# A planner's table of engine costs re-fitted: TensorE's rate, fixed parts, GpSimd's rate and an idle clock

## The chip, the core and the metric

The kernel runs on one core of a Trainium2 chip as one program. The metric is the device time of one execution in microseconds, as the median of a few runs. A core has five instruction queues: TensorE (PE in the profile, with its weight loads as PEld), VectorE (DVE), ScalarE (ACT), GpSimd (POOL) and SyncE (SP, here for DMAs alone). Each queue is worked off in the order in which the program holds it.

## The reference, cut to what matters

A two-layer diffusion backbone in float32, with 512 latent tokens (`x`) and 256 context tokens (`ctx`), 1024 wide, FFN width 2816. Each layer is a half-step SwiGLU FFN, a mixer, and a second half-step FFN, each behind a modulated RMSNorm:

```python
mod_l = (silu(c) @ w_mod[i] + b_mod[i])          # 9 x 1024, the same for ctx with c_ctx
x = x + 0.5 * mod[2] * swiglu(modulate(rmsnorm(x), mod[0], mod[1]), w13, w2)
x = x + mod[5] * mixer(modulate(rmsnorm(x), mod[3], mod[4]))
x = x + 0.5 * mod[8] * swiglu(modulate(rmsnorm(x), mod[6], mod[7]), w13, w2)
```

The mixer of layer 0 is a bidirectional S5 state-space scan beside a multi-scale pooling of windows; that of layer 1 is a bidirectional gated DeltaNet of 8 heads in chunks, with a triangular solve for each chunk. At the end stands a final RMSNorm of `x`.

## The kernel before

The work is one long stream of weight slabs (128 x 1024), in the order of the layers. SP loads a slab, ACT rounds it to the matmul's format (`whi`), DVE or POOL forms what the rounding left (`wlo`), and PE multiplies it in three passes (`whi` by `hhi`, `whi` by `hlo`, `wlo` by `hhi`) with tokens as columns. Stages in order of the span: first FFN (to about 640 us), S5 and pooling mixer (to about 960), second FFN of layer 0 and first of layer 1 (to about 2000), DeltaNet mixer (to about 2660), last FFN. The FFNs after the first use seven products in place of eight, with extra sums on DVE.

Beside the main stream run side threads. In the first FFN one makes the modulation rows (`mods`, L535: a row of 1024 products with a sum, tile `mscr` on DVE, started at least `MP` = 5000 ns apart, L69, L584 and L2608; 56 rows for two streams), and one builds the S5 tables (`tables`, L1307: tiles `z` and `s5u` on DVE and POOL, then transposes of `z` and products on PE). In the DeltaNet mixer (`mixer1`, L1906) the main thread projects 24 tiles, then 8 more, while threads work on each head: `conv` (L2049, DVE; tiles `kT`, `qT`, `sqsum`), `norms` (L2075; `kn` scaled on POOL), `pre` (L2125; loads `E`, masks it on POOL, makes the matrices `NT` and `aq`), `subst` and `loop` (L2209 and L2241; a triangular substitution of 31 steps with two POOL instructions each, `s5l` and `xm`), `levels` (L2288; tiles `fX`, `fP`, `fQ` on 32 or 64 partitions) and four `scan` threads (L2363; tiles `u`, `O`, in a chain of PE, DVE and ACT).

No order is written out by hand. Class `Flow` (L78) is a list planner that runs while the program is built. Each stage is a Python generator. `run` (L237) always goes on with the thread that can start first, by the planner's own clock; what that thread issues is appended to the engines' queues, so the order of these calls is the program order of every queue. Each issued instruction passes through `engine` (L197, the call at L206, which is why every instruction of the profile has this line) to `account` (L130). There the instruction starts when its engine is free and its operands are ready (`ready`, L121: the end of the write plus a hop from `HOP`, L87: 197 ns after PE, 142 after ACT, 127 after DVE, 105 after POOL), and takes `c` ns from a table by engine, operation, size and type. `account` sees all of PE, ACT, DVE, POOL and DMAs; the result changes no instruction, only what is called next. `flag` (L460) lets a thread go on only when what it needs is done by the planner's PE time, and the free PSUM bank is chosen by planned use (L297). Some waits are numbers in planner time: the pace of the modulation rows above, `MPS` = 9000 for those of layer 1.

The two lines of the table that price PE and POOL are these:

```python
c = max(n / 2.4 * (1 if ins[-1].dtype == F32R else 2 if op == "transpose" else 4), 27.0)
c = n * 0.83 + 140.0 if op == "affine_select" else n / 1.2 + 60.0 if op == "memset" else n * 2.05 + 145.0
```

Here `n` is the number of elements in a partition of the output. The functions that the diff touches follow.

Of the kernel before, what the change touches and what calls it, by code (L numbers as in the profile page):

```python
# [11 lines left out]
F32R = mybir.dt.float32r  # L12
# [6 lines left out]
P = 128  # L19
# [58 lines left out]
class Flow:  # L78
# [11 lines left out]
    def __init__(self):  # L90
        self.free = dict.fromkeys(("tensor", "scalar", "vector", "gpsimd", "sync"), 0.0)
        self.dma = self.sent = 0.0
        self.writes = {}
        self.bank_of = {}
        self.bank_used = [0.0] * 8
        self.held = [False] * 8
        self.chunk_banks = []
        self.flags = {}
        self.threads = []
        self.now = self.end = 0.0  # L100
        self.table = 0
        self.first = {}
        self.cost = {}
        self.used = self.last = self.uset = None
        self.tabs = {}
# [24 lines left out]
    def account(self, eng, op, a, k):  # L130
        self.used = self.used or eng
        aps = [v for v in (*a, *k.values()) if isinstance(v, bass.AP)]
        outs = [aps[0]] + ([k["accum_out"]] if k.get("accum_out") is not None else [])
        ins = [v for v in aps[1:] if v is not k.get("accum_out")]
        t = max(self.free[eng], *(self.ready(v, eng) for v in aps))
        n = 1
        for s in aps[0].shape[1:]:
            n *= s
        if op == "dma_start":
            b = 4.0  # L140
            for s in aps[0].shape:
                b *= s
            if eng == "gpsimd":
                self.free[eng] = t + 1040.0
                t += 1040.0
            else:
                self.free[eng] = t + 60.0
                t += 1100.0
            self.dma = max(self.dma, t) + b / 360.0
            self.sent = self.dma + 900.0  # L150
            self.note(aps[0], self.sent, "dma")
            return
        banks = [self.bank_of[v.tensor.name] for v in aps if v.tensor.name in self.bank_of]
        if eng == "tensor":
            c = max(n / 2.4 * (1 if ins[-1].dtype == F32R else 2 if op == "transpose" else 4), 27.0)
        elif eng == "scalar":
            c = n / 1.2 + (51.0 if ins[0].tensor.name in self.bank_of else 93.0)
            c += 93.0 * (len(outs) > 1 or isinstance(k.get("scale"), bass.AP) or isinstance(k.get("bias"), bass.AP))
            s = self.TABLE.get(k.get("func", a[2] if len(a) > 2 else None))
            self.uset = self.uset or s  # L160
            if s and s != self.table:
                self.table = s
                c += 1283.0
        elif eng == "vector":
            m = 1
            for s in ins[0].shape[1:] if ins else ():
                m *= s
            two = op in ("tensor_tensor", "tensor_add", "tensor_sub", "tensor_mul", "tensor_max")
            c = max(n, m) / 0.96 + (69.0 if two or len(ins) < 2 else 130.0)
            if op == "scalar_tensor_tensor" and not isinstance(a[2] if len(a) > 2 else k.get("scalar"), bass.AP):  # L170
                c -= 61.0
            if op in ("tensor_scalar", "tensor_copy") and not banks:
                c -= n / 1.92
        else:
            c = n * 0.83 + 140.0 if op == "affine_select" else n / 1.2 + 60.0 if op == "memset" else n * 2.05 + 145.0
        t += c
        self.free[eng] = t
        for v in outs:
            self.note(v, t, eng)
        for b in banks:  # L180
            self.bank_used[b] = max(self.bank_used[b], t)
        if t > self.end:
            self.end, self.last = t, eng
# [2620 lines left out]
```

## Time and profile before

| what | value |
|---|---|
| runs, us | 3003.7, 2997.89, 3007.39 (median 3003.7) |
| profiled execution, us | 2999.02 |
| its span, us | 2997.2 |
| mean granted TensorE clock | 0.968 |
| PE / DVE / ACT / POOL busy, share of span | 93% / 69% / 41% / 24% |
| HBM read, written | 308.10 MB, 45.25 MB |

The profile shows one execution. A line of it names engine, operation, output tile, input tiles, how often, busy time and mean time of one, then the idle time of the engine before these instructions and who ended it. "PE ps <- POOL kn" among the waits means that PE stood idle, with a matmul that writes a PSUM tile next in its queue, until POOL had written `kn`. The granted clock is a share of full speed.

### The profile page before, as it was taken

The numbers are of one execution on the slowest core, as the hardware profiler recorded it, in microseconds if no ns is written. First come the engines' busy times: TensorE is split into PE (matmuls) and PEld (weight loads), VectorE is DVE, ScalarE is ACT, GpSimd is POOL, SyncE is SP. The second block draws the span as 40 slices with busy tenths as digits, with TensorE's granted clock in tenths as the row PEclk, the third lists the DMA queues.
The fourth block names the chain that finished last, engine by engine and source line by source line (L and its number), as shares of the span: only waits on it lengthen the run. The fifth ranks groups of instructions, "written<-read, shape, count | busy, mean of one in ns | idle before, by whom it ended". The sixth has DMA issues, their size and how long they took to land.

```text
span 2997.2 us, 47031 instructions
## 1 busy us (share of the span) xinstructions
PE 2774.2 (93%) x18380; PEld 2520.0 (84%) x18380; DVE 2060.3 (69%) x3941; ACT 1242.2 (41%) x2464; POOL 708.5 (24%) x1210
## 2 busy tenths in 40 slices
PE   7999989999999999999999999998778888889998
PEld 3787778888888999988999998897667777789977
DVE  6878763256837788753779895367667776678845
ACT  3221212224336444422544443236665766455532
POOL 1244521031212000010201111022764474100011
PEclk9999999999999999999999999999889999899999
DMA  6544442222421544442155665222111133224441
GB/s 233 164 158 163 154 143 70 65 68 82 120 55 41 197 157 146 164 152 79 43 185 168 211 231 202 80 81 88 47 43 49 34 103 114 102 75 134 139 160 57
DMA packets 99247, 356.41 MB, mean 119 GB/s; under 512 B 12448, under 2 KB 16192, under 8 KB 97360
## 3 DMA queue, kind: packets, MB, share of 16 engines
q1 hardware_dynamic: 57552, 192.12, 19.5%
q0 software_dynamic: 38144, 157.09, 15.8%
q10 hardware_dynamic: 3328, 4.20, 0.4%
q8 instruction: 144, 2.36, 0.3%
q14 instruction: 79, 0.65, 0.1%
HBM read 308.10 MB, written 45.25 MB: 118 GB/s over the span
## 4 chain that ended last, share of the span: by engine, by line
PE 66%; DVE 10%; POOL 9%; issue 6%; DMA 6%; ACT 3%; POOLq 0%; DVEq 0%; SPq 0%; ACTq 0%
PE ps L206 66%; POOL xm L206 2%; POOL s5l L206 2%; POOL z L206 2%; DMA E<-gd 2%; DVE wlo L206 1%; POOL s5u L206 1%; DVE mscr L206 1%; DMA wf<-in_wmodf_dram 1%; DVE xT L206 1%; DMA grffn<-gdffn 1%; DVE rsq_a L206 1%; DVE nt L206 1%; DMA z<-in_s5c_dram 1%; DVE h7l L206 1%
## 5 line engine op out<-in xcount | busy, mean ns | idle before, releaser
L206 DVE TENSOR_TENSOR wlo<-raw,whi 128x1024 fp32r<-128x1024 f32 (+1 forms) x310 | 352.3, 1138 | 352.6 <-ACT whi L206 351.9
L206 ACT ACTIVATE whi<-raw 128x1024 fp32r<-128x1024 f32 (+1 forms) x324 | 316.0, 978 | 652.3 <-PE ps L206 641.9
L206 PE MATMUL ps<-hhi,whi 128*128 128x256 f32 (+1 forms) x1304 | 457.3, 351 | 0.5 <-ACT gg L206 0.5
L206 PE MATMUL ps<-hlo,whi 128*128 128x256 f32 (+1 forms) x1304 | 441.0, 338 | 1.4 <-DVE hlo L206 1.4
L206 PE MATMUL ps<-hhi,wlo 128*128 128x256 f32 (+1 forms) x1304 | 440.1, 337 | 2.0 <-DVE wlo L206 1.4
L206 PE MATMUL ps<-h7h,whi 128*128 128x256 f32 (+1 forms) x976 | 298.6, 314 | 4.6 <-ACT whi L206 4.0
L206 PE MATMUL ps<-h7h,wlo 128*128 128x256 f32 (+1 forms) x976 | 297.4, 313 | 4.9 <-DVE wlo L206 4.8
L206 PE MATMUL ps<-ghffn,wlo 128*128 128x256 f32 (+1 forms) x896 | 296.3, 331 | 5.5 <-DVE wlo L206 5.5
L206 PE MATMUL ps<-h7h,sh 128*128 128x384 f32 (+1 forms) x960 | 293.3, 318 | 6.9 <-ACT cffn L206 6.8
L206 PE MATMUL ps<-ghffn,whi 128*128 128x256 f32 (+1 forms) x896 | 297.5, 332 | 0.4 <-ACT ghffn L206 0.4
L206 PE MATMUL ps<-glffn,whi 128*128 128x256 f32 (+1 forms) x896 | 297.2, 332 | 0.6 <-DVE glffn L206 0.6
L206 PE MATMUL ps<-h7h,sl 128*128 128x384 f32 (+1 forms) x960 | 293.1, 317 | 3.4 <-DVE sl L206 3.4
L206 DVE SCALAR_TENSOR_TENSOR xT<-ps,gate,xT 128x256 f32<-128x256 f32 (+1 forms) x352 | 195.1, 578 | 128.3 <-PE ps L206 124.0
L206 PEld LDWEIGHTS ps<-hhi,wlo 128*128 128x128 f32 x1304 | 251.2, 193 | 31.3 <-DVE wlo L206 1.8
L206 PEld LDWEIGHTS ps<-hhi,whi 128*128 128x128 f32 x1304 | 252.2, 193 | 27.0 <-issue 1.2
L206 PEld LDWEIGHTS ps<-hlo,whi 128*128 128x128 f32 x1304 | 252.5, 194 | 25.0 <-DVE hlo L206 2.0
L206 PE MATMUL ps<-h7l,whi 128*128 128x256 f32 (+1 forms) x976 | 217.9, 313 | 2.1 <-DVE h7l L206 2.1
L206 ACT ACTIVATE cffn<-ps 128x384 f32<-128x384 f32 (+1 forms) x300 | 131.7, 451 | 197.6 <-PE ps L206 196.4
L206 POOL TENSOR_TENSOR sqsum<-sqsum,sq 128x256 f32<-128x256 f32 x96 | 78.2, 815 | 557.8 <-ACT sq L206 476.4
L206 PEld LDWEIGHTS ps<-h7h,wlo 128*128 128x128 f32 x976 | 188.2, 193 | 6.0 <-DVE wlo L206 5.7
L206 PEld LDWEIGHTS ps<-h7h,whi 128*128 128x128 f32 x976 | 188.2, 193 | 5.5 <-ACT whi L206 4.4
L206 PEld LDWEIGHTS ps<-ghffn,wlo 128*128 128x128 f32 x896 | 169.2, 189 | 23.7 <-DVE wlo L206 6.7
(350 smaller groups left out, 6396.3 us busy)
## 6 DMA issues: line engine op xcount, KB each, us to landing
raw<-in_ffn_dram SPq DMA_DIRECT2D x264, 512.0 KB
xT<-in_wmod_dram POOLq DMA_DIRECT2D x72, 512.0 KB, 4.6
wm<-in_wmod_dram POOLq DMA_DIRECT2D x56, 512.0 KB, 4.2
raw<-in_gin_dram SPq DMA_DIRECT2D x33, 512.0 KB
grffn<-gdffn POOLq DMA_DIRECT2D x40, 384.0 KB, 4.2
gdffn<-cffn POOLq DMA_DIRECT2D x36, 384.0 KB, 2.6
wf<-in_wmodf_dram POOLq DMA_DIRECT2D x16, 512.0 KB, 7.9
xd<-xT POOLq DMA_DIRECT2D x2, 3072.0 KB, 11.1
```

The costliest lines, as they stand in the source:

```text
L206: r = f(*a, **k)
```

## The change

Only the planner's table is changed, and one field is added. No instruction, tile, wait or DMA is added or taken out; what can change is the order of the instructions in each queue, and the times in planner time at which paced steps come up.

- PE: products in the rounded format go from N/2.4 to N/2.2 ns, doubled below 256 columns; float32 products get 10 ns more and a floor of 54 in place of 27; transposes go from N/1.2 with that floor to N/1.2 + 3 with a floor of 30.
- PE when idle: after more than 3400 ns without an instruction, everything that starts in the 4500 ns that follow is priced twice.
- ACT: the fixed part goes from 51 to 78 ns with a PSUM source, from 93 to 113 otherwise; 110 more on fewer than 128 partitions.
- DVE: 18 ns more for each instruction, 90 more on fewer than 128 partitions, 350 more for a transpose of 512.
- POOL: two-operand instructions go from 2.05 N + 145 to 2.5 N + 200, selects from 0.83 N + 140 to N + 168, memsets from N/1.2 + 60 to N + 72.

Hops, DMA prices and paces stay as they are.

```diff
--- before.py
+++ after.py
@@ -97,7 +97,7 @@
         self.chunk_banks = []
         self.flags = {}
         self.threads = []
-        self.now = self.end = 0.0
+        self.now = self.end = self.cold = 0.0
         self.table = 0
         self.first = {}
         self.cost = {}
@@ -152,9 +152,18 @@
             return
         banks = [self.bank_of[v.tensor.name] for v in aps if v.tensor.name in self.bank_of]
         if eng == "tensor":
-            c = max(n / 2.4 * (1 if ins[-1].dtype == F32R else 2 if op == "transpose" else 4), 27.0)
+            if op == "transpose":
+                c = max(n / 1.2 + 3.0, 30.0)
+            elif ins[-1].dtype == F32R:
+                c = n / 2.2 * (2 if n < 256 else 1)
+            else:
+                c = max(n / 0.6 + 10.0, 54.0)
+            if t - self.free[eng] > 3400.0:
+                self.cold = t + 4500.0
+            if t < self.cold:
+                c *= 2
         elif eng == "scalar":
-            c = n / 1.2 + (51.0 if ins[0].tensor.name in self.bank_of else 93.0)
+            c = n / 1.2 + (78.0 if ins[0].tensor.name in self.bank_of else 113.0) + (110.0 if aps[0].shape[0] < P else 0.0)
             c += 93.0 * (len(outs) > 1 or isinstance(k.get("scale"), bass.AP) or isinstance(k.get("bias"), bass.AP))
             s = self.TABLE.get(k.get("func", a[2] if len(a) > 2 else None))
             self.uset = self.uset or s
@@ -171,8 +180,9 @@
                 c -= 61.0
             if op in ("tensor_scalar", "tensor_copy") and not banks:
                 c -= n / 1.92
+            c += 18.0 + (90.0 if aps[0].shape[0] < P else 0.0) + (350.0 if op == "transpose" and n == 512 else 0.0)
         else:
-            c = n * 0.83 + 140.0 if op == "affine_select" else n / 1.2 + 60.0 if op == "memset" else n * 2.05 + 145.0
+            c = n + 168.0 if op == "affine_select" else n + 72.0 if op == "memset" else n * 2.5 + 200.0
         t += c
         self.free[eng] = t
         for v in outs:
```

## Rows read from the trace of the kernel before

**Rows 1.** The page, part 1: busy us (share of span) and instructions of each engine.
```profile
PE 2774.2 (93%) x18380; PEld 2520.0 (84%) x18380; DVE 2060.3 (69%) x3941; ACT 1242.2 (41%) x2464; POOL 708.5 (24%) x1210
```

**Rows 2.** Stretches: from:to, length, busy us (instructions), granted clock, DMA share, GB/s.
```profile
60.00:440.00 380.00, 350.51 (x2114) 303.27 (x2113) 311.51 (x555) 87.71 (x138) 146.68 (x177) 0.97 0.48 155
440.00:640.00 200.00, 200.00 (x1210) 175.51 (x1209) 69.09 (x98) 43.67 (x64) 14.80 (x20) 1.00 0.22 70
1050.00:1250.00 200.00, 200.00 (x1152) 200.00 (x1151) 174.47 (x266) 89.01 (x139) 16.65 (x31) 1.00 0.44 147
2000.00:2680.00 680.00, 559.61 (x4459) 495.26 (x4458) 482.90 (x1042) 412.39 (x1091) 303.68 (x642) 0.92 0.22 74
2100.00:2250.00 150.00, 116.81 (x1032) 102.34 (x1033) 99.23 (x207) 97.33 (x268) 102.26 (x221) 0.85 0.13 44
2700.00:2840.00 140.00, 140.00 (x1213) 140.00 (x1213) 123.09 (x188) 82.62 (x145) 7.02 (x13) 1.00 0.41 132
```

**Rows 3.** Waits of PE in 60:440: us in total, times, longest us.
```profile
PE ps L206 <- DVE z L206: 17.9, 6, 6.3
PE ps L206 <- POOL z L206: 9.5, 5, 2.5
```

**Rows 4.** Waits of PE in 2000:2680, columns as before.
```profile
PE ps L206 <- POOL kn L206: 20.0, 5, 7.7
PE ps L206 <- DVE u L206: 17.9, 6, 8.4
PE ps L206 <- ACT qT L206: 16.0, 1, 16.0
PE ps L206 <- DVE O L206: 8.3, 5, 4.4
PE ps L206 <- ACT u L206: 7.3, 5, 2.9
PE ps L206 <- DVE NT L206: 6.9, 2, 4.5
PE ps L206 <- ACT O L206: 5.8, 7, 1.6
PE ps L206 <- ACT fQ L206: 2.6, 1, 2.6
PE ps L206 <- DVE fP L206: 1.9, 3, 0.7
```

**Rows 5.** POOL by shape, 2050:2550: count, busy us, mean ns, idle before it.
```profile
L206 POOL TENSOR_SCALAR_AFFINE_SELECT E<-E 128x768 f32<-128x768 f32 x16 | 16.2, 1014 | 66.5 <-DMA E<-gd 66.5
L206 POOL TENSOR_TENSOR s5l<-lm,xm 128x126 f32<-128x126 f32 x24 | 14.0, 583 | 1.7
L206 POOL TENSOR_TENSOR s5l<-lm,xm 128x120 f32<-128x120 f32 x16 | 11.8, 740 | 1.0
L206 POOL TENSOR_TENSOR s5l<-lm,xm 128x110 f32<-128x110 f32 x16 | 8.9, 558 | 1.0
L206 POOL TENSOR_TENSOR kn<-kn,rsq_r 128x768 f32<-128x768 f32 x8 | 12.6, 1580 | 21.5 <-DVE rsq_r L206 21.5
```

**Rows 6.** POOL by shape, 60:440, columns as in rows 5.
```profile
L206 POOL TENSOR_TENSOR z<-z,s5u 128x128 f32<-128x128 f32 x14 | 13.7, 980 | 1.0
```

**Rows 7.** DVE and ACT by shape, 2000:2680, columns as in rows 5.
```profile
L206 DVE SCALAR_TENSOR_TENSOR u<-ps,neG,nv 128x128 f32<-128x128 f32 x80 | 26.7, 345 | 19.6 <-PE ps L206 18.7
...
L206 ACT ACTIVATE u<-ps 128x128 f32<-128x128 f32 x112 | 28.6, 273 | 37.4 <-PE ps L206 37.0
L206 ACT ACTIVATE fX<-lm 32x192 f32<-32x192 f32 x48 | 17.3, 360 | 9.4 <-DVE lm L206 8.6
```

**Rows 8.** DVE by shape, 60:440, columns as in rows 5.
```profile
L206 DVE SCALAR_TENSOR_TENSOR mscr<-wm,cbc 128x1024 bf16<-128x1024 f32 x112 | 147.7, 1319 | 16.1 <-DMA wm<-in_wmod_dram 14.4 <-DVE gg L206 0.4 <-ACT cbc L206 0.2
L206 DVE DVE_READ_ACCUMULATOR mscr<-wm,cbc 128x1 f32 x112 | 9.2, 82 | 0.0
```

**Rows 9.** The chain that ended last, 2060:2240: shares of the stretch by line.
```profile
by line: PE ps L206 25.5%; issue 15.3%; POOL xm L206 15.3%; POOL s5l L206 15.0%; DMA E<-gd 13.4%; DVE wlo L206 2.9%; POOL E L206 2.9%; POOL kn L206 2.4%; DVE NT L206 2.3%; DVE sqsum L206 1.8%; DVE lm L206 1.6%; DVE qT L206 1.1%; DVE aq L206
```

## The prediction

> **What bounds the kernel now.** I read the page's busy line first, then the stretches by stage, then what TensorE (PE) waits for in the stages where it stands idle, then the durations of the instructions behind those waits. The busy line shows PE at 93% of 2997.2 us [rows 1], so 223 us of the span have no matmul in flight, and only this part can move: the diff changes no instruction, only the order in which each engine's queue holds them. The stretches show where the idle time is [rows 2]. In 440-640, 1050-1250 and 2700-2840 PE is busy for the whole stretch at a granted clock of 1.00: no other order can help there. In the first FFN (60-440) PE is busy 350.5 of 380 us, so 29.5 us are idle. In the DeltaNet mixer (2000-2680) it is busy 559.6 of 680 us, so 120 us are idle, and the granted clock is 0.92 there, 0.85 in 2100-2250. What is left, about 73 us, lies in the first 60 us, in the norms between stages and at the end, where a chain has nothing beside it.
>
> What PE waits for in these two stretches is not the stream of weights but side work that stands in its queue ahead of ready matmuls. In the first FFN it is the S5 tables: 17.9 us for z from VectorE (DVE) and 9.5 us for z from GpSimd (POOL) [rows 3], almost all of the 29.5. In the mixer it is the heads' chains: kn from POOL 20.0, u 17.9, qT 16.0, O 8.3 and so on, 86.7 us in the nine rows that stand here [rows 4]. PE takes its queue in order, so each is a place where the planner thought that the side chain would be done by the time PE got there. That is what the table of costs decides.
>
> **The change part by part.**
>
> *PE's rate* (N/2.4 to N/2.2 columns per ns). In 1050-1250 the matmuls have 384 columns: 1152 in 200 us, 173.6 ns each, 2.21 columns per ns; in 2700-2840 they have 256: 1213 in 140 us, 115.4 ns each [rows 2]. The old table says 160 and 106.7, the new one 174.5 and 116.4. The new one is right within 1%, the old one 8% short. In saturated stretches this changes nothing in time (cost 0; what hides it is that PE never waits there, and without that cover a slab split laid later would show as a wait of PE on wlo, of which these stretches have none; I keep 0). Elsewhere it means that the planner counts 9% fewer main matmuls passing during a side chain of given length, so a side chain's own PE steps move forward in PE's queue unless the chain's prices rise as much.
> The Trainium skill's page "TensorE: Matmul & The Clock Gate", section "Back-to-back issue gap", gives N/2.4 + 2.5 ns for an isolated matmul at the full clock: 162.5 ns for 384 columns. By that rule the old rate would be the right one, the new table would make PE 7% too slow and bring its side steps too early, and the time would be that of the slower rival below. The 173.6 ns measured speak against it.
>
> *Fixed parts of ScalarE (ACT) and DVE.* A scan link on DVE (u, 128 columns) goes from 263 to 281 and with its unchanged hop of 127 from 390 to 408, 4.6% more; one on ACT (u from PSUM) from 158 to 185, with its hop of 142 from 300 to 327, 9% more. Measured are 345 and 273 [rows 7], busy time alone. So these chains rise by about as much as PE or a little less: relative to PE nothing moves. I take 0 for the waits on u and O (17.9 + 8.3 + 7.3 + 5.8 = 39.3 us [rows 4]); the bounds are half of them gone (-20) and half as much again (+20). The waits on qT (16.0) I leave as they are: one wait, and its chain is of this kind.
>
> *POOL, and tiles on fewer than 128 partitions.* A loop step s5l of 126 elements goes from 403 to 515; measured 583 [rows 5]. That closes 112 of 180 ns, 62%. kn (768) goes from 1719 to 2120, measured 1580: from short to long, which only lays the steps behind it later. The ACT copies of 32 partitions (fX, 192) go from 253 to 383, measured 360 [rows 7]. So for the chains that run through these, the planner now sees most of the delay that it missed, by more than PE's 9%, and lays their PE steps behind more of the projections. The PE waits that hang on them are kn 20.0, NT 6.9, fQ 2.6 and fP 1.9, 31.4 us [rows 4]. I take 62% of them: -19.5 us. Bounds: all the 86.7 us of the group gone, or +20. What is late next where such a wait goes: the matmuls that moved ahead are projections, whose tiles wait for a free pad buffer, so the fill can run out, and the chain itself gets no faster. In 2060-2240 it runs through the POOL loop for 30% (xm 15.3, s5l 15.0) and through the E transfers for 13% [rows 9]; POOL stands 66.5 us before E's selects for those [rows 5], and the transfers' price is not changed. So the gain is bounded by the waits and doesn't reach the chain.
>
> *The S5 tables in the first FFN.* POOL's z of 128 goes from 407 to 520, measured 980 [rows 6]: 113 of 573 ns, 20%. I take 20% of the 9.5 us: -2 us. For the 17.9 us behind DVE's z I take 0, since DVE's +18 ns and PE's 9% pull against each other. Bounds: all 27.4 gone, or +10.
> For POOL the rows show a price that is not one of size: s5l takes 583 at 126 elements, 740 at 120 and 558 at 110 [rows 5]. The Trainium skill's page "SBUF — State Buffer", section "Who interferes with whom", says that a DVE instruction with two SBUF inputs contends with a GpSimd instruction that reads SBUF. By that rule POOL's time hangs on what DVE does beside it, no price per size can place the loop's end, and the waits would stay: the no-change rival. The rows agree that the price varies.
>
> *The pace of the modulation rows.* 56 rows start at least 5 us apart in the table's time, while the matmuls between them cost 9% more of that time: they get packed into fewer matmuls. Their DVE time is 147.7 + 9.2 = 156.9 us [rows 8], in a stretch where DVE is busy 311.5 of 380 us, 82% [rows 2]. Squeezed into 350 us that is 89%, still under full; cost 0, bounds 0 and +10.
>
> *The idle clock* doubles PE's prices for 4.5 us after an idle time over 3.4 us, and *DVE's 512 transpose* gets 350 ns. Few waits in the rows are that long (8.4, 7.7 and 16.0 us at the longest [rows 4]); cost 0, inside the bounds of the mixer.
>
> Sum: -19.5 - 2 = -21.5 us. The profiled execution took 2999.0 us (span 2997.2); less 21.5 it is 2977.5. The median of the three runs, 3003.7, lies 4.7 above the profiled one, so I forecast **2982 us**, 0.7% faster. What a measurement of this kernel can tell from no change is about 0.3%, 9 us.
>
> **The rivals.**
> 1. *No change*: orders change only where PE is saturated, and the waits stay because their causes are not in the table (E's transfers, POOL's varying price). For: the chain's 13% on E [rows 9], the spread of s5l [rows 5]. Against: the loop's step is now priced 28% higher (403 to 515) and a 32-partition copy 51% (253 to 383), far more than PE's 9%, so the orders of the mixer will not stay. Time 3004, within 9. Chance 0.20. That the change doesn't do what it says belongs here.
> 2. *Slower, in the scan*: DVE's links rise 4.6% and PE 9%, so the scan's PE steps (u, aq, S) stand earlier in PE's queue by some 4% of the chain, while a link measures 345 ns busy against 281 in the new table [rows 7]. It decides where the table still undershoots the link by more than the old PE rate gave as slack, 8%; 345 against 281 is 19% under. Then the 39.3 us of waits on u and O [rows 4] grow by half, +20 us, and PE loses some 3 more at a granted clock of 0.85 [rows 2] (20 x 0.15): 2999.0 + 23 + 4.7 = 3027. For: the table stays short on exactly these links. Against: ACT's links rise with PE. Chance 0.27.
> 3. *Much faster*: half of all the waits of both stretches go, (86.7 + 27.4) / 2 = 57 us: 2999.0 - 57 + 4.7 = 2947. For: PE, DVE, ACT and POOL all come nearer to the trace. Against: z at 520 for 980 [rows 6]. Chance 0.11.
>
> **How the numbers follow.** The forecast (9 to 40 us faster) has 0.42, much faster 0.11, so faster has 0.53; same 0.20; slower 0.27. The range goes from 2942 (past rival 3, of which it leaves out a part) to 3024 (most of rival 2); some 0.1 is left out on each side. Of the likeliest case alone it would be 2962 to 2994.
>
> **What would show it.** Right: in 2000-2680 PE's idle time falls from 120 to about 100 us, the wait on kn falls to a third or less and NT, fQ and fP with it, the granted clock there rises above 0.92; saturated stretches keep 173.6 and 115.4 ns per matmul; the first FFN keeps its waits on z. Wrong: the waits on u and O grow (rival 2), E's transfers end as late as before and the mixer keeps its 680 us (rival 1), or the waits on z go too (rival 3). A mixer as long as before with PE's waits gone would mean that the chain sets the end, and that the step from waits to time has failed.

## The result and the profile after

The changed kernel takes **3021.3 us** (median of 5 runs, 3017.7 to 3028.2) against 3003.9 of the kernel before (5 runs): ratio **1.0062 [1.0042, 1.0081]**, 0.6% slower. The forecast was 2982, 0.7% faster; the time lies inside the range (2942 to 3024), on the other side. The profiled execution shown below took 3025.3 us, its span 3023.6.

The page's busy line of the changed kernel, beside [rows 1]: the same instructions but for two table loads of ACT, each engine within 1% of its busy time. PE is busy 22.0 us longer (2774.2 before), which is most of the 26.4 us by which the span grew.

```profile
PE 2796.2 (92%) x18380; PEld 2532.5 (84%) x18380; DVE 2062.7 (68%) x3941; ACT 1248.1 (41%) x2466; POOL 711.0 (24%) x1210
```

**Where the time went.** I took the start of the first matmul of a slab as a milestone in both traces. The first FFN ends (slab 66) at 666 us before and 663 after. The DeltaNet mixer begins (slab 217) at 2000 and 2001. At slab 264, the seventh of the last FFN, the traces stand at 2666 and 2690, and at the end 26 us apart. (The expectations below that speak of the first slab of the last FFN mean this slab 264.) So the whole loss arises between slabs 217 and 264, +23 us; "mixer" means this stretch from here on. Inside it the lead changes: at slab 240, among the last projections, the changed kernel is 21 us ahead, and from there to slab 264 it loses 45.

The stretches of the changed kernel, columns as in [rows 2]:

```profile
60.00:440.00 380.00, 355.24 (x2149) 307.79 (x2149) 311.85 (x561) 88.90 (x140) 139.93 (x180) 0.97 0.49 157
1050.00:1250.00 200.00, 200.00 (x1152) 200.00 (x1151) 173.15 (x266) 87.78 (x138) 16.13 (x30) 1.00 0.46 156
2000.00:2690.00 690.00, 565.31 (x4346) 492.74 (x4346) 472.15 (x1022) 409.26 (x1079) 315.71 (x640) 0.89 0.21 70
2725.00:2865.00 140.00, 140.00 (x1213) 140.00 (x1213) 123.11 (x187) 83.10 (x145) 7.01 (x13) 1.00 0.41 131
```

The same milestones in the kernel before, same columns:

```profile
2000.00:2666.00 666.00, 545.61 (x4338) 481.26 (x4337) 471.37 (x1024) 404.01 (x1076) 302.60 (x640) 0.92 0.22 73
```

The saturated stretches keep 173.6 ns (200 us / 1152) and 115.4 ns (140 / 1213) per matmul. In the mixer PE's idle time grows by little, from 120.4 to 124.7 us; its busy time for almost the same number of matmuls grows by 19.7, at a granted clock of 0.89 in place of 0.92. The clock records of the two traces put 113 us of this stretch at the lower level (1.2 in place of 2.4 GHz) before and 147 after. By an estimate, 34 us more at half the pace cost 17, most of the 19.7. So the longer stage is paid here mostly as slower matmuls, and the table of PE's waits shows only the smaller part.

The waits of PE in 60:440, then in 2000:2700, of the changed kernel (us in total, times, longest), beside [rows 3] and [rows 4]:

```profile
PE ps L216 <- POOL z L216: 12.5, 5, 4.7
PE ps L216 <- DVE z L216: 10.1, 4, 4.3
...
PE ps L216 <- POOL kn L216: 21.3, 6, 7.4
PE ps L216 <- DVE O L216: 16.6, 10, 5.3
PE ps L216 <- ACT oTh L216: 12.4, 5, 6.1
PE ps L216 <- DVE u L216: 11.4, 10, 4.2
PE ps L216 <- POOL pad L216: 8.5, 1, 8.5
PE ps L216 <- ACT qT L216: 8.3, 1, 8.3
PE ps L216 <- ACT u L216: 7.5, 4, 3.1
PE ps L216 <- ACT cffn L216: 7.3, 1, 7.3
PE ps L216 <- DVE sq L216: 6.7, 1, 6.7
PE ps L216 <- ACT fQ L216: 6.1, 3, 3.9
...
PE ps L216 <- ACT O L216: 2.0, 4, 0.8
```

NT has all but left the list (0.3 us), but kn, the largest term of my sum, stands at 21.3 where it was 20.0. The four rows of that term (kn, DVE's NT, fQ, DVE's fP) come to 28.1 us where they were 31.4. The four rows of u and O come to 37.5 us (39.3 before).

**What got longer is a chain on GpSimd.** GpSimd works eight triangular loops, one per head, in one in-order queue; the last mixer matmuls follow the last loop. The last loop ends at 2516 before and 2540 after, and slab 264 follows 150 us later in both. (In the other runs below it follows 121 to 165 us later, so the end of the last loop is a sign of the mixer's length and doesn't set it alone.) The tile `s5l` of the changed kernel, first and last start at the end:

```profile
L216 POOL TENSOR_TENSOR s5l<-lm,xm x248: 215/406/1571, 2100.3 to 2539.4; 128x126 f32<-128x126 f32 x12, 128x30 f32<-128x30 f32 x8, 128x56 f32<-128x56 f32 x8, 128x78 f32<-128x78 f32 x8
```

What blocks the loops is the mask of the decay matrix `E` of a later head, a POOL instruction that the planner placed between two steps of a loop. POOL's timeline in the loop of head 2, kernel before (start, length, then in brackets the idle time before it and who ended it):

```profile
2211.44 0.42 POOL L206 TENSOR_TENSOR xm<-xm,s5l 128x120 f32<-128x120 f32 x1
2218.99 0.97 POOL L206 TENSOR_SCALAR_AFFINE_SELECT E<-E 128x768 f32<-128x768 f32 x1 [7.13 <-DMA E<-gd]
2219.94 0.40 POOL L206 TENSOR_TENSOR s5l<-lm,xm 128x121 f32<-128x121 f32 x1
```

The same place in the changed kernel:

```profile
2203.80 0.43 POOL L216 TENSOR_TENSOR xm<-xm,s5l 128x126 f32<-128x126 f32 x1
2219.15 0.98 POOL L216 TENSOR_SCALAR_AFFINE_SELECT E<-E 128x768 f32<-128x768 f32 x1 [14.91 <-DMA E<-gd]
2220.10 0.43 POOL L216 TENSOR_TENSOR s5l<-lm,xm 128x136 f32<-128x136 f32 x1
```

`E` of head 3 lands at 2219 in both. Before, its mask stands behind step 20 of the loop and blocks it for 7.1 us; after, it stands behind step 14 and blocks it for 14.9. The loop takes 39.5 us before and 53.4 after. Summed over POOL's idle times directly before a mask inside the eight loops (those of 0.5 us or more), it is 18.8 us before and 34.9 after; the loops' own steps take 237 and 250 us, the gaps between loops 103 and 97. So of the 24 us by which the last loop ends later, 16 are waits before masks; 13 are slower steps of the same number and size, and the gaps give 6 back.

Why the mask moved can be followed in the planner's own clock. There is one buffer for each direction of `E`; DVE's `aq` of head 2 reads it last, so the load of head 3 can't start before `aq` is done. `account` prices a load from SP's own planned free time and doesn't ask whether its buffer is free: in the changed plan `E` of head 3 is issued at 2058.6 and has landed at 2063.8, while `aq` of head 2 ends only at 2110.2. So the mask is planned 1.1 us after `aq`. In the trace the first `aq` of head 2 ends at 2212.56, SP issues the load at 2212.63, and the mask starts at 2219.15, 6.6 us after `aq`:

```profile
2211.87 1.29 DVE L216 TENSOR_TENSOR aq<-ps,E 128x512 f32<-128x512 f32 x2 [1.41 <-PE ps L216]
2212.63 1.22 SPq L216 DMA_DIRECT2D E<-gd  x2
```

That error is the same in both tables. New is that a loop step costs 28% more (403 to 515 ns), so the planner thinks that fewer steps have run by the time `aq` is done, and puts the mask, with its unpriced wait, further ahead in the loop.

### The profile page after: what moved, and what is told of

Its sections match the earlier page's. It is cut to its first block, busy times and chain, and to the rows that moved or that the text cites. A ratio compares the mean times of both kernels' runs of the same rounds, so it can differ in the third digit from the quotient of the medians.

```text
span 3023.6 us, 47045 instructions
## 1 busy us (share of the span) xinstructions
PE 2796.2 (92%) x18380; PEld 2532.5 (84%) x18380; DVE 2062.7 (68%) x3941; ACT 1248.1 (41%) x2466; POOL 711.0 (24%) x1210
## 4 chain that ended last, share of the span: by engine, by line
PE 66%; DVE 11%; POOL 8%; issue 7%; DMA 5%; ACT 3%; DVEq 0%; POOLq 0%; SPq 0%; ACTq 0%
PE ps L216 66%; POOL xm L216 2%; POOL s5l L216 2%; DVE mscr L216 1%; POOL z L216 1%; DVE wlo L216 1%; DVE xT L216 1%; DMA E<-gd 1%; DMA xT<-in_x_dram 1%; DMA og<-ogd 1%; DVE rsq_r L216 1%; DMA z<-in_s5c_dram 1%; DMA grffn<-gdffn 1%; POOL s5u L216 1%; DVE rsq_a L216 1%
## 5 line engine op out<-in xcount | busy, mean ns | idle before, releaser
L216 PEld LDWEIGHTS ps<-h7h,sh 128*128 128x128 f32 x960 | 181.6, 189 | 10.4 <-ACT cffn L216 10.4
```

What stands on the lines that cost most here:

```text
L216: r = f(*a, **k)
```

## Experiments

Each run's median and ratio stand against the kernel before on the same chip (its medians: 3001.0 to 3003.5). The other columns come from the run's profiled execution and its trace: the difference to before at slab 66 (end of the first FFN), that between slabs 217 and 264 (mixer), POOL's idle time before masks inside the loops, and the end of the last loop, counted from the start of the span (so it moves with the first FFN too).

| run | us | ratio [interval] | slab 66 | mixer | masks in loops | last loop ends |
|---|---|---|---|---|---|---|
| (before) | 3003.9 | | 0 | 0 | 18.8 | 2516 |
| (after) | 3021.3 | 1.0062 [1.0042, 1.0081] | -3 | +23 | 34.9 | 2540 |
| pe_only | 3026.2 | 1.0076 [1.0061, 1.0091] | +24 | +1 | 13.9 | 2539 |
| pool_only | 3028.3 | 1.0084 [1.0069, 1.0099] | +4 | +24 | 44.2 | 2538 |
| fixed_only | 3050.4 | 1.0158 [1.0141, 1.0175] | -7 | +37 | 16.8 | 2604 |
| one_ns | 3014.4 | 1.0036 [1.0023, 1.0049] | -2 | +13 | 21.0 | 2532 |
| old_act1 | 3007.5 | 1.0012 [1.0001, 1.0023] | -1 | +7 | 18.2 | 2522 |
| old_pool1 | 3028.9 | 1.0084 [1.0055, 1.0113] | -1 | +30 | 17.6 | 2559 |
| new_dve1 | 3026.9 | 1.0077 [1.0048, 1.0106] | -3 | +23 | 40.2 | 2565 |
| new_act1 | 3021.8 | 1.0047 [1.0023, 1.0072] | -6 | +22 | 30.4 | 2550 |
| new_e8 | 3002.5 | 0.9999 [0.9990, 1.0009] | -3 | +3 | 2.9 | 2512 |
| old_e8 | 3013.6 | 1.0035 [1.0022, 1.0048] | 0 | +14 | 0.0 | 2527 |
| new_aq3 | 3016.2 | 1.0041 [1.0027, 1.0055] | -5 | +16 | 23.1 | 2519 |
| old_aq3 | 3016.2 | 1.0041 [1.0027, 1.0054] | -1 | +16 | 15.5 | 2529 |
| new_e8_act1 | 3002.2 | 1.0008 [0.9997, 1.0018] | -2 | -1 | 2.8 | 2503 |
| new_e8_dve1 | 3000.8 | 0.9995 [0.9986, 1.0005] | -8 | -1 | 0.0 | 2509 |
| old_e8_act1 | 3001.9 | 1.0006 [0.9997, 1.0016] | +1 | +3 | 0.0 | 2519 |
| new_e8_z | 2984.0 | 0.9941 [0.9926, 0.9956] | -26 | +3 | 0.0 | 2489 |
| new_e8_z_og | 2975.7 | 0.9913 [0.9898, 0.9928] | -26 | -5 | 0.0 | 2487 |
| old_e8_z_og | 2972.2 | 0.9910 [0.9892, 0.9928] | -38 | +8 | 0.0 | 2490 |

Names with "old" have the table of before, those with "new" the changed one. Three theories go into the runs. By the first, the "loop theory" of the expectations, the loops are longer because masks wait inside them for a landing of `E` that has no price, and POOL's new prices moved those masks. By the second, their "chance theory", there is no single cause: the order of before is a lucky one, and any redraw loses. By the third, their "fill theory", PE's higher price draws projections forward and leaves PE nothing to do beside the last heads. The scan's waits on u and O (my rival 2) are out by the rows above.

**One part of the change at a time.** pe_only has PE's new prices without the idle clock, in the old table:

```diff
-            c = max(n / 2.4 * (1 if ins[-1].dtype == F32R else 2 if op == "transpose" else 4), 27.0)
+            if op == "transpose":
+                c = max(n / 1.2 + 3.0, 30.0)
+            elif ins[-1].dtype == F32R:
+                c = n / 2.2 * (2 if n < 256 else 1)
+            else:
+                c = max(n / 0.6 + 10.0, 54.0)
```

pool_only has POOL's new prices alone:

```diff
-            c = n * 0.83 + 140.0 if op == "affine_select" else n / 1.2 + 60.0 if op == "memset" else n * 2.05 + 145.0
+            c = n + 168.0 if op == "affine_select" else n + 72.0 if op == "memset" else n * 2.5 + 200.0
```

fixed_only has the fixed parts of ACT and DVE alone:

```diff
-            c = n / 1.2 + (51.0 if ins[0].tensor.name in self.bank_of else 93.0)
+            c = n / 1.2 + (78.0 if ins[0].tensor.name in self.bank_of else 113.0) + (110.0 if aps[0].shape[0] < P else 0.0)
...
+            c += 18.0 + (90.0 if aps[0].shape[0] < P else 0.0) + (350.0 if op == "transpose" and n == 512 else 0.0)
```

> Only PE's prices are changed (rate, float32, transposes). In the changed kernel the whole loss lies in the DeltaNet mixer, and the first slab of the last FFN follows the end of the last POOL loop by 150 us there as before. Loop theory (the E selects stand inside the POOL loops before E has landed and block them): here the select of head 3 stands at step 29 of loop 2, behind step 20 of before, and nothing blocks more than before: 2990 to 3008 us, E's waits inside the loops at most 19 us. Fill theory (PE priced slower draws projections forward and leaves nothing beside the tail): slower, 3013 to 3025. Chance theory (any new order moves the mixer by some 10 us either way): anything from 2990 to 3020, with no relation to the E selects.

> Only POOL's prices are changed. The select of head 3 stands at step 7 of loop 2 (before: 20; changed kernel: 14), that of head 5 at step 12 of loop 4. Loop theory: blocked longer than in the changed kernel, E's waits inside the loops 35 to 50 us, 3018 to 3035 us. Fill theory: PE's price is as before, so 2995 to 3010. Chance theory: 2990 to 3020.

> Only the fixed parts of ACT and DVE are changed. The select of head 3 stands at step 26 of loop 2 (before: 20). Loop theory: E's waits inside the loops as before or less, 2992 to 3008 us. Fill theory: PE relatively faster, 2990 to 3004. Chance theory: 2990 to 3020.

Every part alone is slower than before, by 0.8, 0.8 and 1.6%; pool_only as the first theory had it (3018 to 3035), the other two not (at most 3008). The sum of the three is five times the loss of all together, so the effects of the entries don't add; how much of that is their pulling against each other and how much the luck of four orders, these runs don't separate. The third theory is out: pe_only, with PE's price alone, loses 1 us in the mixer, and pool_only, without it, loses 24.

pe_only has no loss in the mixer, as the loops would have it (masks 13.9 us); its loss is in the first FFN, +24 us. PE's waits there in 60:440:

```profile
PE ps L211 <- POOL z L211: 29.6, 8, 5.8
PE ps L211 <- DVE z L211: 11.2, 5, 4.4
```

With PE priced 9% dearer and POOL as before, the steps on `z` move forward in PE's queue: by the records of the traces the last of them has 1791 slab matmuls ahead of it, where it had 2064 before. The wait on POOL's `z` rises from 9.5 [rows 3] to 29.6; the waits on both `z` grow by 13 us, and the granted clock of 60:440 falls from 0.97 to 0.94. In the whole change the last step on `z` stands behind 2091 slab matmuls and the wait is 12.5: the other entries take the shift back. Alone, POOL's prices lay it behind 2091, the fixed parts behind 2187. No change by 1 ns below moves the end of this FFN by more than about 5 us, so this loss is more than luck.

pool_only has the mixer's loss by itself. POOL's timeline in the loop of head 2:

```profile
2207.09 0.39 POOL L206 TENSOR_TENSOR xm<-xm,s5l 128x100 f32<-128x100 f32 x1
2223.85 1.41 POOL L206 TENSOR_SCALAR_AFFINE_SELECT E<-E 128x768 f32<-128x768 f32 x1 [16.37 <-DMA E<-gd]
```

Here only POOL's steps are dearer, the rest of the plan is not, and the mask stands behind step 7. Masks block the loops for 44.2 us, the most of all runs. The loss of 24 us alone would prove little, since old_pool1 below loses 30 by 1 ns.

fixed_only is a miss. Inside the loops it waits less than before (16.8), and it still loses 37 us in the mixer, with 168 us of gaps between loops (103 before), and 29 us more between slabs 66 and 217. Its POOL waits in 2060:2610 show long waits before loops, which the theory of masks inside them doesn't cover (masks waited 66.5 us in all before [rows 5]):

```profile
POOL E L207 <- DMA E<-gd: 105.8, 7, 26.1
POOL s5l L207 <- DVE lm L207: 40.2, 1, 40.2
POOL pad L207 <- DVE kT L207: 37.4, 2, 24.2
```

Ahead of the mixer PE's waits on DVE's `sl` and `wlo` grow from 5.6 to 21.0 us; what else makes up the 29 us stays open.

**How much is the luck of one order?** A list planner may come out with another order for any small change. These five change one hop by 1 ns, which makes no price truer or falser: that of DVE from 127 to 128 (one_ns on the old table, new_dve1 on the new), that of ACT from 142 to 143 (old_act1, new_act1), that of POOL from 105 to 106 (old_pool1). The first:

```diff
-    HOP = {"tensor": 197.0, "scalar": 142.0, "vector": 127.0, "gpsimd": 105.0, "dma": 0.0, "bank": 60.0}
+    HOP = {"tensor": 197.0, "scalar": 142.0, "vector": 128.0, "gpsimd": 105.0, "dma": 0.0, "bank": 60.0}
```

> Only the hop after DVE is changed, from 127 to 128 ns: a price that is neither more nor less true, so whatever it does is what a new order does by itself. Loop theory: the select of head 3 stands at step 24 of loop 2 (before: 20), that of head 5 at step 1 of loop 4 (before: 0): within 6 us of before, 2998 to 3010. Fill theory: 3000 to 3008. Chance theory: off by 8 us or more in the mixer alone, either way.

> The old table with the hop after ACT at 143 in place of 142 ns: no truer, no falser; it reshuffles the mixer from the fourth head on. Chance theory (before holds a favourable draw of the mixer's order; every redraw loses, whichever table it comes from): mixer (first slab of the stage to first slab of the last FFN) 676 to 700 us against 666 of before, time 3010 to 3030. Table theory (the new prices are worse for this planner): within 8 us of before, 2995 to 3012.

> The old table with the hop after POOL at 106 in place of 105 ns. Chance theory: mixer 676 to 700 us, time 3010 to 3030. Table theory: within 8 us of before, 2995 to 3012.

> The new table with the hop after DVE at 128 in place of 127 ns; the mixer is the same as in the changed kernel up to the fourth head. Chance theory: mixer 676 to 700 us, time 3008 to 3035, no worse than the redraws of the old table. Table theory: 3018 or more, 15 us or more above the redraws of the old table.

> The new table with the hop after ACT at 143 in place of 142 ns. Chance theory: mixer 676 to 700 us, time 3008 to 3035, no worse than the redraws of the old table. Table theory: 3018 or more, 15 us or more above the redraws of the old table.

The old table gives 3002 to 3004, 3007, 3014 and 3029 us, the changed one 3021, 3022 and 3027. The kernel before is the best of the old table's four orders: 1 ns costs it 4 to 25 us. So a part of the 0.6% is what any redraw would be likely to lose, and whether the new table is worse than the old on average isn't shown by so few. Two things are stable: all three orders of the new table lose 22 to 23 us in the mixer, with masks in the loops at 30 to 40 us, and no order of the old table has more than 21 us of masks. The converse doesn't hold: old_pool1 loses 30 us with 17.6 of masks, its gaps between loops at 133 us and its steps at 251. one_ns and old_pool1 came out as the second theory had it, old_act1 not (3007, where it had 3010 to 3030). Masks in loops are one cause of a long mixer, not the only one.

**Pricing the landing of E.** If the loss is the unpriced wait, it goes when the planner issues the masks only 8 us (planner time) after the load; if it is the luck of the draw, it stays for some draws. Both tables, then neighbours by 1 ns as above (new_e8_act1, new_e8_dve1, old_e8_act1):

```diff
                     E1 = load(hd + 1)
+                if hd:
+                    yield flow.now + 8000.0
                 for d in range(2):
```

> The changed kernel, with one price more: the planner waits 8 us of its time between the load of E for a head and E's selects on POOL (the trace shows 6 to 7 us from the load's issue to the end of the select, and the planner's own DMA clock lets E land at once). Nothing else is edited. Loop theory (POOL stands inside its loops before E has landed, 34.9 us in the changed kernel against 18.8 before, and the last loop's end sets the mixer's): idle time before E inside the loops under 12 us, the last loop ends at 2505 to 2530 (changed kernel: 2540), time 2995 to 3012. Chance theory: the idle time falls, but the last loop ends at 2525 to 2560 all the same, time 3010 to 3035.

> The same price of 8 us in the kernel before. Loop theory: idle time before E inside the loops falls from 18.8 to under 8 us, the last loop ends at 2500 to 2516, time 2988 to 3004. Chance theory: a redraw of a favourable order, time 3008 to 3030.

> new_e8 with the hop after ACT at 143 in place of 142 ns, which reshuffles the mixer from the fourth head on. If pricing E is a cure: idle time before E inside the loops stays under 8 us, the last loop ends at 2500 to 2525, time 2992 to 3012. If new_e8 was a lucky redraw: like the redraws of the changed kernel, 3015 to 3030.

> new_e8 with the hop after DVE at 128 in place of 127 ns, a smaller reshuffle. Cure: idle time before E under 8 us, 2995 to 3010. Lucky redraw: 3012 to 3030.

> old_e8 with the hop after ACT at 143 in place of 142 ns. If the old table loses by its own prices when E is priced: 3010 to 3022, as old_e8. If old_e8 was one bad order: 2994 to 3008, as the redraws of new_e8.

With this one line the changed kernel is level with the kernel before (0.9999), and so are both neighbours (1.0008, 0.9995). POOL's waits in 2090:2515 of new_e8:

```profile
POOL s5l L216 <- DVE lm L216: 59.4, 3, 22.3
POOL s5l L216 <- DMA xm<-in_unitx_dram: 28.6, 1, 28.6
POOL pad L216 <- DVE kT L216: 9.4, 1, 9.4
POOL s5l L216 <- ACT modv L216: 6.8, 1, 6.8
POOL kn L216 <- DVE rsq_r L216: 6.0, 1, 6.0
POOL E L216 <- DMA E<-gd: 4.2, 2, 2.9
```

The same view of the changed kernel, 2090:2545, has three rows on `E`:

```profile
POOL E L216 <- DMA E<-gd: 50.3, 5, 21.8
POOL E L216 <- DVE rsq_r L216: 31.1, 2, 23.3
...
POOL E L216 <- DVE rsq_a L216: 4.4, 1, 4.4
```

In the three waits that the last two rows put down to DVE, the landing of `E` too came only 0.1 to 0.2 us before the mask started, so they count as waits for `E` here. Masks then wait 4.2 us in place of 85.8; 2.9 of it lies inside loops (34.9 by the sum above). POOL's other waits grow from 61.3 to 110.5 us, so a part of the time comes back elsewhere. The last loop ends 28 us earlier, the mixer is 20 us shorter. PE's wait on kn is 21.3, 16.9 and 14.1 us in the three orders without the line and 11.3, 12.4 and 6.1 in the three with it. So with this price the loss of the change is gone, in three orders of its table out of three, and without it all three have it. On the old table the line gives one bad order (3014, a miss of the first theory, which had 2988 to 3004) and one level one (3002): 18.8 us of waits before masks go there and nothing is gained. A wait before a mask is thus not worth its length in time by itself, and why the old table gains nothing stays open.

**A third buffer instead.** If `aq` with a third buffer lets the chain of the heads run freer, both kernels gain; the wait on two scans back becomes one on three:

```diff
-                if hd >= 2:
+                if hd >= 3:
                     for d in range(2):
-                        yield ("scan", hd - 2, d)
-                Q = R["aq"] = [ht(f"aq{d}", [P, 4, P], 2) for d in range(2)]
+                        yield ("scan", hd - 3, d)
+                Q = R["aq"] = [ht(f"aq{d}", [P, 4, P], 3) for d in range(2)]
```

> The changed kernel with three buffers for aq in place of two, so that head h waits for the scan of head h-3 and not h-2 before it makes aq, frees E earlier and loads E of the next head earlier. This takes the cause of E's lateness away, not its price. Loop theory: E has landed before its selects come up in POOL's queue, idle time before E inside the loops under 12 us, the last loop ends 15 to 35 us earlier than in the changed kernel, time 2985 to 3006. If the chain from the scan of head h-3 over kn to the loop of head h sets the pace, and not E: the last loop ends within 10 us of the changed kernel's 2540, time 3010 to 3030.

> The kernel before with three buffers for aq. Loop theory: the last loop ends 10 to 20 us earlier than 2516, time 2983 to 2996. If the chain over kn sets the pace: 2998 to 3015.

Both come out at 3016.2: 5 us below the changed kernel, 13 above the one before beside which they ran. That is inside what 1 ns does, so these two runs say nothing for or against the buffer but that it is no cure; the first theory had expected a gain from both.

**The same mistake elsewhere.** If missing prices are the point and not rates, pricing the others should beat both kernels. new_e8_z adds to new_e8 a price fitted to POOL's `z` (1.8 N + 730 ns: 960 at 128 elements, measured 980 [rows 6]) and 3 us before the transposes of DVE's `z`. new_e8_z_og also takes the store of a head's output off SP, where it stands in order ahead of loads that are ready. old_e8_z_og has the same three edits on the old table.

```diff
+            if aps[0].tensor.name.startswith(("z", "s5u")):
+                c = n * 1.8 + 730.0
...
+                            yield self.flow.now + 3000.0
                             for ri in range(2):
...
-                nc.sync.dma_start(ogd[hd], on)
+                nc.scalar.dma_start(ogd[hd], on)
```

> new_e8, with POOL's price for the S5 tables' z and s5u at 1.8 N + 730 ns (960 at 128, where the trace shows 980 and the new table has 520), and 3 us of planner time more before the transposes of DVE's z. The mixer's order is that of new_e8. Price theory (PE stands before z because z is priced too cheap): PE's waits on z in the first FFN fall from 22 to 26 us to under 8, the first FFN ends 12 to 25 us earlier, time 2978 to 2992. Rival (the first FFN is held by DVE, busy at 82%, and a wait that goes comes back as another): the first FFN within 6 us, time 2996 to 3008.

> new_e8_z with the heads' outputs stored from ACT's queue in place of SP's, where a store that waits for a scan stands before loads that are ready (the unit matrix of the next head came up to 28 us late in new_e8). If these blocks lie on the chain of the loops: the mixer 5 to 15 us shorter than in new_e8_z, time 2965 to 2988. If the chain over kn sets the pace, or by a redraw: within 12 us of new_e8_z either way, 2978 to 3004.

> The old table with the same three edits as new_e8_z_og (E's landing, z's price, the stores on ACT's queue). If the new prices help once nothing else is missing: 2984 to 3004, at least 8 us above new_e8_z_og's 2976. If the table's PE, ACT, DVE and POOL prices are worth nothing here: 2966 to 2984. In the first FFN, where z stands on both with the same price: PE 9% too cheap lays z's steps later still, waits on z under 8 us, the stage 20 to 30 us shorter than before.

PE's waits on z in 60:440 of new_e8_z, where they were 22.6 us in the changed kernel:

```profile
PE ps L218 <- DVE z L218: 4.5, 5, 1.8
PE ps L218 <- POOL z L218: 1.7, 2, 1.3
```

Against new_e8 PE waits 20 us less for `z` (26.3 there), the first FFN ends 23 us earlier, and the kernel takes 18 us less (2984.0): in this stage PE is the bound, and waits did turn into time. The store of the outputs was the cause of the 28.6 us row of new_e8 above: in 2220:2266 SP waited for the output of a head, and the loads of `E` and of the unit matrix stood behind that store.

```profile
SPq L216 <- ACT O L216: 44.0, 2, 31.1
```

With the store on ACT's queue, POOL's row on the unit matrix is gone and the kernel takes 2975.7 us; 8 us less is no more than a redraw can give, so what the store costs in time isn't shown. The old table with the same edits takes **2972.2**: the intervals overlap. In 60:440 PE waits for z no more at all there:

```profile
PE ps L208 <- DVE wlo L208: 1.4, 1, 1.4
PE ps L208 <- ACT gg L208: 0.5, 1, 0.5
PE ps L208 <- DVE hlo L208: 0.2, 1, 0.2
```

Both beat both kernels, by 0.9% against before. Each is one order without a neighbour by 1 ns; the part in the first FFN (26 and 38 us) is more than any such neighbour moved. With the missing prices in, the re-fitted rates are worth nothing that these runs can tell.

## Why the prediction was wrong, point by point

- **PE's rate: right.** 173.6 and 115.4 ns stayed, and the saturated stretches lost or gained nothing. The Trainium skill's page "TensorE: Matmul & The Clock Gate", section "Back-to-back issue gap", gives for an isolated matmul N/2.4 + 2.5 ns, by an estimate 162.5 ns for 384 columns; in these streams the trace of after disagrees as that of before did. The sentence that side steps move forward "unless the chain's prices rise as much" is what pe_only showed: z's steps moved forward, and the stage took 24 us more.
- **Fixed parts of ACT and DVE, 0 +- 20: right in sum for the whole change** (u and O 39.3 to 37.5 us), in part by luck: DVE's u fell from 17.9 to 11.4 while DVE's O rose from 8.3 to 16.6. The wait on qT, which I left as it was, halved (16.0 to 8.3). And 0 is not a property of the part: alone it cost 48 us in all. "Relative to PE nothing moves" is true only with PE's new price beside it.
- **POOL and narrow tiles, -19.5: the step that failed.** It failed twice. The wait on kn didn't fall (20.0 to 21.3, the four rows 31.4 to 28.1) though POOL's step was priced better: what ends late is the loop, and what lengthens it is first the landing of `E` (16 us), whose price the change leaves at nothing, then slower steps (13 us). And I turned PE's waits into time in a stage where PE isn't the bound: its idle time there rose by 4 us, its busy time by 20, though the prediction starts from the sentence that only the idle time can move. I had the facts in my rows: the chain's 13% on `E` [rows 9], the 66.5 us of POOL before masks [rows 5], and the sentence "the gain is bounded by the waits and doesn't reach the chain". From that sentence the term should have been 0 at best, and the question should have been what a dearer loop step does to the place of an instruction that waits for an unpriced transfer. That place moved from step 20 to 14, and the stage grew by 23 us; with the landing priced the 23 became 3.
- **The S5 tables, -2: right in sum, by luck**, -3 us at slab 66, waits 27.4 to 22.6. POOL's z, whose wait was to fall by 2, rose from 9.5 to 12.5, and DVE's, taken as unchanged, fell from 17.9 to 10.1. That most of the 27.4 us was to be had, by a price for POOL's z and a delay before DVE's, new_e8_z showed (6.2 left).
- **Modulation rows: right**, DVE 311.9 us busy in 60:440 (311.5 before), and PE waits for none of them.
- **Idle clock: not tested apart.** pe_only left it out, and no run has the change without it; its share stays open.
- **The rivals.** Rival 2 had the sign and nearly the size (3027), but not the cause: u and O didn't grow. Rival 1 named the cause, `E`'s transfers, and took it for a reason that nothing would change; an unpriced wait is not neutral when the prices around it move. Rival 2's rule for the clock, 15% of 20 us, was far too small: of the mixer's 24 us only 4 are idle time of PE.
- **The chances.** The forecast gave an aimed gain of 0.7% to a change that redraws all orders. With 1 ns costing the kernel before 4 to 25 us, any redraw of it would have been likely to be slower; these runs came after the forecast.

## What to carry to other kernels

In a planner with a table of costs look first for waits that it prices at nothing (a load whose buffer is still in use, a queue held up by a store ahead) before refining rates, since a truer rate beside a missing price can move an in-order instruction to a worse place, as POOL's did here. Turn PE's waits into time only in a stage where PE is the bound; elsewhere follow the chain that ends the stage. And set any reorder against a redraw that means nothing, such as 1 ns on one entry, before crediting it to what was changed.

## What the hardware showed that I had not expected

- A load of `E` (128 x 768 f32 with rows repeated over partitions) takes 6.5 us from its issue on SP, 2212.63, to the start of the mask that waits for it, 2219.15 [the changed kernel's timelines]. Over the heads of both kernels whose first mask waited it is 6.3 to 8.6 us.
- In new_e8 one store that waited 31.1 us for its data in SP's queue kept back a load of the unit matrix behind it, whose reader then stood 28.6 us.
- POOL's loop steps of one size differ by 2.4 times. In one loop of the changed kernel, steps of 120 to 135 elements follow each other at 0.4 and at 1.0 us:

```profile
2473.66 1.00 POOL L216 TENSOR_TENSOR s5l<-lm,xm 128x120 f32<-128x120 f32 x1
2474.75 0.42 POOL L216 TENSOR_TENSOR xm<-xm,s5l 128x120 f32<-128x120 f32 x1
```

Beside the slow ones DVE runs five instructions with two large inputs (771 elements), one row of its timeline; they end where the steps turn fast again:

```profile
2468.95 5.45 DVE L216 SCALAR_TENSOR_TENSOR sqsum<-pad,vecs,sqsum 128x771 f32<-128x771 f32 x5
```

The row ends at 2474.4. This agrees with the Trainium skill's page "SBUF — State Buffer", section "Who interferes with whom", by which a DVE instruction with two SBUF inputs contends with a GpSimd instruction that reads SBUF; no run here took that DVE work away, so it is read and not shown.
